# Sums of squares in transposed 32-blocks on VectorE, and factors spread by DMA, in a two-layer trunk on one core

## The chip, the cores and the metric

One core of one Trainium2 chip. The metric is device time in microseconds, the median of the runs. The kernel before takes 2295.11 us (three runs, 2294.74 to 2296.44).

## The reference

Two layers over 512 rows of width 2048, all in float32. Each layer normalises h, multiplies by one wide projection, feeds its columns to three mixers (latent attention A, sparse attention B, differential attention C), gates their outputs, multiplies by an output projection, and adds a gated embedding. The change is about the inner RMS norms: those of the two latents of mixer A, and that of each of the five heads of mixer C.

```python
def rms_norm(x, g):
    y = xf * lax.rsqrt(jnp.mean(xf * xf, axis=-1, keepdims=True) + NORM_EPS)
    return (y * g.astype(jnp.float32)).astype(x.dtype)
...
    q = (rms_norm(c_q, q_norm_g) @ w_uq).reshape(b, s, A_HEADS, A_NOPE + A_ROPE)
    kv = (rms_norm(c_kv, kv_norm_g) @ w_ukv).reshape(b, s, A_HEADS, A_NOPE + A_V)
...
    o = rms_norm(o, subln_g) * (1.0 - lam_init)
```

## The kernel before

Activations lie transposed: features on the 128 partitions, the 512 rows of the sequence (tokens) along the free axis. A norm over features is therefore a sum over partitions. Every float32 operand of a large product is split into a high part (ScalarE, L260 or L263) and a low part (VectorE, L261 or L264), and each product is three matmuls (`mm3`, L358 to L360).

The main loop runs over 15 groups of columns of the input projection (L931). Each group reads its weights in 8 chunks (`chunk`, L338): a DMA on the queue of SyncE (SP) into one of 3 buffers `wr`, then splits into `wh` and `wl` (4 buffers each). The mixers are Python generators that `pump` (L400) steps between the products of a group, by a budget in microseconds that each `yield` states. A scheduler then sets the order of the instructions on each engine by its own timeline; each engine executes its list in that order, and so does each DMA queue.

The square norms are made so. `col_sums` (L308) takes a 128x512 tile of squares and multiplies each 128x128 block of it, as the stationary operand, with two columns of ones: 4 matmuls of float32, each two instructions. The sums come out with the token on the partition. `rsqrt` (L316) makes 1/sqrt of them by ScalarE's Sqrt and a Newton step on VectorE. `spread` (L330) transposes a broadcast of each of the 4 columns, 4 more matmuls, and leaves in PSUM a 128x512 tile with the factor of each token in every partition.

Seven such norms stand in a layer. `latents` (L650) does one for cq (three tiles) and one for ckv (two tiles): squares, `col_sums`, `rsqrt`, `spread`, then z times the factor (L666) and a split with the gain (L667, which runs L263 and L264). The products with `w_uq` (L696) use cq, those with `w_ukv` (`nope_key` and the values, L700 to L717) use ckv. For mixer C, `diff_after` (L825) copies the column sums of each head into `csum`, and after the fifth head takes `rsqrt` of all 20 columns. `gate` (L900) reads a head's output back from DRAM (L905) and multiplies by `spread` of its 4 columns (L908), many groups later.

The queue of GpSimd (POOL) carries the writes to DRAM, that of SP the weights and the reads back. Tiles of 128x512 come from a pool of 59 slots (`slot`); `at` is one of four PSUM banks.

```python
        def latents(kind, n, size, gain, res):
...
            yield GAP
            r = sm(4)
            rsqrt(r, col_sums(total), 4, size)
            yield 0.45
            yield GAP
            rb = spread(r)
            for j in range(n):
                DVE.tensor_tensor(zs[j], zs[j], rb, op=ALU.mult)
                res.append(split(zs[j], col(gain + j)))
```

Of the kernel before, what the change touches and what calls it, by code (L numbers as in the profile page):

```python
# [24 lines left out]
EPS = 1e-6  # L25
# [173 lines left out]
def trunk(ctx: ExitStack, tc: tile.TileContext, t, out):  # L199
# [53 lines left out]
    identb = const.tile([128, 128], BF16, name="identb")  # L253
    DVE.tensor_copy(identb, identf)
    onesf = const.tile([128, 2], F32, name="onesf")
    DVE.memset(onesf, 1.0)
# [47 lines left out]

    mean = const.tile([128, 4 * C_H], F32, name="mean")
    corr = const.tile([128, 4 * C_H], F32, name="corr")

# [7 lines left out]

    def rsqrt(dst, src, n, size):  # L316

        y, m, e = dst[:, :n], mean[:, :n], corr[:, :n]
        o = 0
        for x in src if isinstance(src, list) else [src]:  # L320
            DVE.tensor_scalar(mean[:, o:o + x.shape[1]], x, 1.0 / size, EPS, op0=ALU.mult, op1=ALU.add)
            o += x.shape[1]
# [262 lines left out]
    for L in range(DEPTH):  # L585
# [24 lines left out]
        def take(nm):  # L610
            nonlocal wi
            kind, j = nm
            if kind in ("vb", "vc", "v5"):
# [9 lines left out]
                if kind == "v5":  # L623
                    wi = const.tile([128, NB, 8], F32, name=f"wi{L}")
                    for b in range(NB):
                        DVE.tensor_scalar(wi[:, b], z[nm][b][:, 256:264], rcol[:, b:b + 1], None, op0=ALU.mult)
# [21 lines left out]


        def latents(kind, n, size, gain, res):  # L650
            zs = [raw.pop((kind, j)) for j in range(n)]
# [7 lines left out]
            yield GAP  # L659
            r = sm(4)  # L660
            rsqrt(r, col_sums(total), 4, size)
            yield 0.45
            yield GAP
            rb = spread(r)
            for j in range(n):
# [125 lines left out]

        csum = const.tile([128, 4 * C_H], F32, name=f"csum{L}")

        def diff_needs(x):
# [30 lines left out]
        def diff_after(x, s):  # L825
            DVE.tensor_copy(csum[:, 4 * x:4 * x + 4], col_sums(s))
            yield 0.45
            if x == C_H - 1:
                rsqrt(csum, csum, 4 * C_H, 128)
                done.add(("csum", 0))  # L830

# [68 lines left out]
        def gate(kind, x):  # L900
# [5 lines left out]
            if kind == "gc":  # L906
                finish(("csum", 0))
                DVE.tensor_tensor(o, o, spread(csum[:, 4 * x:4 * x + 4]), op=ALU.mult)  # L908
                DVE.scalar_tensor_tensor(o, o, sub_c[:, L:L + 1], s, op0=ALU.mult, op1=ALU.mult)
            else:  # L910
                DVE.tensor_tensor(o, o, s, op=ALU.mult)
# [194 lines left out]
```

## Time and profile before

| | |
|---|---|
| runs, median (lowest to highest) | 2295.11 us (2294.74 to 2296.44) |
| profiled execution, its own time | 2295.42 us |
| its span, first to last instruction | 2293.6 us |
| granted TensorE clock, mean | 0.997 |
| busy: TensorE (PE), its weight loads (PEld) | 2272.2 us, 1913.0 us |
| busy: VectorE (DVE), ScalarE (ACT), GpSimd (POOL) | 1366.9 us, 1006.9 us, 114.9 us |
| DMA | 268.33 MB, mean 117 GB/s |

A busy share is the time in which an engine had an instruction under way. Durations of matmuls in the profile overlap, since matmuls are pipelined: what one costs is read from the distance between starts, not from its duration. In a timeline each row has its start and its duration in us from the start of the span, and in square brackets how long the engine was idle before it and for whom. "Landing" is the time from a DMA's issue to its last byte.

### The profile page before, as it was taken

The page shows a single profiled execution, that of the slowest core. Times are in us where ns is not written, and L with a number is a line of the kernel's source. Part 1 is how long each engine was busy: PE and PEld are TensorE (multiplying, and loading weights), DVE is VectorE, ACT ScalarE, POOL GpSimd, SP SyncE. Part 2 cuts the span into 40 slices and gives each one's busy share as a digit, 9 for nine tenths or more (in the row PEclk, how much of TensorE's full clock was granted, in tenths as well). Part 3 has the DMA queues.
Part 4 walks back from the last instruction along what each step waited for, and adds up shares of the span by engine and source line. Part 5 has one row for each costly group of instructions (what it writes and reads, how often), then busy time and mean ns, then how long its engine had stood idle before and what let it go on. Part 6 is the DMA issues. An engine that isn't in the chain of part 4 may idle for free.

```text
span 2293.6 us, 29988 instructions
## 1 busy us (share of the span) xinstructions
PE 2272.2 (99%) x10988; PEld 1913.0 (83%) x10988; DVE 1366.9 (60%) x2886; ACT 1006.9 (44%) x1931; POOL 114.9 (5%) x204
## 2 busy tenths in 40 slices
PE   8999999999999999999999999999999999999997
PEld 7898888888888888888888888888888888888887
DVE  7655559977767543344555555699676665333445
ACT  6444445454545432233434444444554454223444
POOL 0000000000000011000000000000000000110003
PEclk9999999999999999999999999999999999999998
DMA  6233323323334345344332333233232243553235
GB/s 201 70 99 116 113 79 96 111 93 97 97 101 161 106 139 185 126 134 136 128 96 76 101 120 104 83 97 102 97 106 102 88 165 115 170 174 130 100 102 165
DMA packets 95220, 268.33 MB, mean 117 GB/s; under 512 B 10976, under 2 KB 26848, under 8 KB 95072
## 3 DMA queue, kind: packets, MB, share of 16 engines
q1 hardware_dynamic: 81760, 223.41, 30.5%
q0 software_dynamic: 13312, 43.00, 5.5%
q8 instruction: 86, 1.41, 0.3%
q14 instruction: 62, 0.51, 0.1%
HBM read 235.96 MB, written 30.41 MB: 116 GB/s over the span
## 4 chain that ended last, share of the span: by engine, by line
PE 98%; ACT 0%; issue 0%; DMA 0%; POOL 0%; SPq 0%; DVE 0%; POOLq 0%; ACTq 0%
PE pp L358 28%; PE pp L359 28%; PE pp L360 28%; PE at L360 3%; PE at L359 3%; PE at L358 3%; PE at L564 2%; PE at L365 1%; PE at L364 1%; PE at L313 1%; PE at L334 0%; DMA x<-in_x_dram 0%; PE at L853 0%; POOL g L1044 0%; ACT wh L260 0%
## 5 line engine op out<-in xcount | busy, mean ns | idle before, releaser
L261 DVE TENSOR_TENSOR wl<-wr,wh 128x512 fp32r<-128x512 f32 (+4 forms) x810 | 530.5, 660 | 731.4 <-ACT wh L260 671.2
L358 PE MATMUL pp<-g,wh 128*128 128x512 f32 (+1 forms) x2432 | 936.0, 386 | 6.2 <-ACT g L263 5.7
L359 PE MATMUL pp<-g,wh 128*128 128x512 f32 (+1 forms) x2432 | 936.1, 385 | 0.0
L260 ACT ACTIVATE wh<-wr 128x512 fp32r<-128x512 f32 (+4 forms) x810 | 487.1, 605 | 978.3 <-PE pp L359 723.9
L360 PE MATMUL pp<-g,wl 128*128 128x512 f32 (+1 forms) x2432 | 911.7, 386 | 0.0
L358 PEld LDWEIGHTS pp<-g,wh 128*128 128x128 f32 x2432 | 457.7, 188 | 94.1 <-ACT g L263 5.7
L359 PEld LDWEIGHTS pp<-g,wh 128*128 128x128 f32 x2432 | 457.6, 188 | 87.5
L360 PEld LDWEIGHTS pp<-g,wl 128*128 128x128 f32 x2432 | 456.7, 188 | 88.6
L359 PE MATMUL pp<-wl,g 128*128 128x512 f32 (+1 forms) x384 | 136.3, 357 | 0.0
L360 PE MATMUL pp<-wh,g 128*128 128x512 f32 (+1 forms) x384 | 135.7, 355 | 0.0
L358 PE MATMUL pp<-wh,g 128*128 128x512 f32 (+1 forms) x384 | 129.3, 363 | 1.2 <-ACT wh L260 1.2
L548 ACT ACTIVATE e<-at,sm 128x128 f32<-128x128 f32 (+3 forms) x128 | 67.0, 525 | 49.5 <-DVE sm L547 48.3
L358 PEld LDWEIGHTS pp<-wh,g 128*128 128x128 f32 x384 | 71.1, 188 | 11.5 <-ACT wh L260 2.1
L360 PEld LDWEIGHTS pp<-wh,g 128*128 128x128 f32 x384 | 72.2, 188 | 9.9
L359 PEld LDWEIGHTS pp<-wl,g 128*128 128x128 f32 x384 | 72.3, 188 | 9.1
L547 DVE TENSOR_REDUCE sm<-at 128x1 f32<-128x128 f32 (+3 forms) x168 | 77.2, 481 | 2.0
L646 POOL DMA_DIRECT2D o_d<-t x32 | 17.4, 542 | 1099.6 <-ACT t L644 1099.6
L261 DVE TENSOR_TENSOR tl<-at,th 128x512 fp32r<-128x512 f32 (+3 forms) x128 | 54.3, 483 | 16.8 <-ACT th L260 16.8
L365 PE MATMUL at<-g 128*128 128x512 f32 (+3 forms) x176 | 53.9, 324 | 0.0
L364 PE MATMUL at<-g 128*128 128x512 f32 (+3 forms) x176 | 53.7, 323 | 0.0
L260 ACT ACTIVATE th<-at 128x512 fp32r<-128x512 f32 (+3 forms) x128 | 45.5, 440 | 18.2 <-PE at L564 18.0
L564 PE MATMUL at<-identf,e 128*128 128x128 f32 x320 | 51.9, 273 | 0.0
(224 smaller groups left out, 2405.2 us busy)
## 6 DMA issues: line engine op xcount, KB each, us to landing
wr<-in_w_in_dram SPq DMA_DIRECT2D x207, 512.0 KB, 3.6
wr<-in_w_pg_dram SPq DMA_DIRECT2D x72, 512.0 KB, 3.7
wr<-in_w_o_dram SPq DMA_DIRECT2D x64, 512.0 KB, 3.7
o_d<-t POOLq DMA_DIRECT2D x32, 256.0 KB, 2.3
g<-o_d SPq DMA_DIRECT2D x32, 256.0 KB, 4.3
hm_d<-t POOLq DMA_DIRECT2D x32, 256.0 KB, 3.2
wr<-in_w_in_dram SPq DMA_DIRECT2D x18, 256.0 KB, 2.6
wr<-in_w_in_dram SPq DMA_DIRECT2D x16, 264.0 KB, 2.6
```

Source lines behind the costliest of these rows:

```text
L260: ACT.activation(hi, src, AF.Copy)
L261: DVE.tensor_tensor(lo, src, f32(hi), op=ALU.subtract)
L313: PE.matmul(ps[:, 2 * b:2 * b + 2], y[:, 128 * b:128 * b + 128], onesf, start=True, stop=True)
L358: PE.matmul(ps, l[0], r[0], start=start, stop=False)
L359: PE.matmul(ps, l[0], r[1], start=False, stop=False)
L360: PE.matmul(ps, l[1], r[0], start=False, stop=stop)
L364: PE.matmul(ps, q[:, qs], k[0][:, :n], start=start, stop=False)
L365: PE.matmul(ps, q[:, qs], k[1][:, :n], start=False, stop=stop)
L547: DVE.tensor_reduce(st[:, 1:2], ps[:, :n], op=ALU.max, axis=AX.X, negate=True)
L548: ACT.activation(e, ps[:, :n], AF.Exp, bias=st[:, 1:2], accum_out=st[:, 2:3])
L564: PE.transpose(ps[:, 128 * (i - kb):128 * (i - kb) + 128], probs[:, BO[i] + 128 * kb:BO[i] + 128 * kb + 128], identf)
L646: nc.gpsimd.dma_start(odram[m], o)
```

## The change

`fold` replaces `col_sums` for the seven inner norms of a layer: VectorE sums each 32x32 block of the squares over rows with a reduce that transposes 32-blocks, which leaves a 128x16 tile; one product with a 128x32 matrix of four stacked identities (`folded`, made once) adds the four groups of 32 partitions. The sums come out as 32x16, and `rsqrt` works on that shape. `put_row` writes the 512 factors to a row in DRAM on POOL's queue, element by element (step 32 in the row), and `get_row` reads the row into all 128 partitions on SP's queue. So `spread` goes from these norms as well. The norms of h and the last norm keep `col_sums` and `spread`. The sums and factors of the five heads are held in one slot in place of `csum`, one row in DRAM each, and are written out after the fifth head.

```diff
@@ -252,6 +252,8 @@
     make_identity(nc, identf)
     identb = const.tile([128, 128], BF16, name="identb")
     DVE.tensor_copy(identb, identf)
+    folded = const.tile([128, 32], F32, name="folded")
+    DVE.tensor_reduce(folded, identf.rearrange("p (a j) -> p j a", j=32), op=ALU.add, axis=AX.X)
     onesf = const.tile([128, 2], F32, name="onesf")
     DVE.memset(onesf, 1.0)
 
@@ -302,8 +304,8 @@
             ACT.activation(s, src, AF.Square)
             DVE.tensor_tensor(acc, acc, s, op=ALU.add)
 
-    mean = const.tile([128, 4 * C_H], F32, name="mean")
-    corr = const.tile([128, 4 * C_H], F32, name="corr")
+    mean4 = const.tile([128, 4], F32, name="mean")
+    corr4 = const.tile([128, 4], F32, name="corr")
 
     def col_sums(y):
 
@@ -313,12 +315,21 @@
             PE.matmul(ps[:, 2 * b:2 * b + 2], y[:, 128 * b:128 * b + 128], onesf, start=True, stop=True)
         return ps[:, 0:2 * nb:2]
 
-    def rsqrt(dst, src, n, size):
-
-        y, m, e = dst[:, :n], mean[:, :n], corr[:, :n]
+    def fold(s):
+
+        part = small.tile([128, 16], F32, name="part", tag="part", bufs=2)
+        DVE.tensor_reduce(part, s.rearrange("p (b j) -> p b j", j=32), op=ALU.add, axis=AX.X, apply_transpose=True)
+        ps = at()
+        PE.matmul(ps[0:32, 0:16], folded, part, start=True, stop=True)
+        return ps[0:32, 0:16]
+
+    def rsqrt(dst, src, n, size, mean=mean4, corr=corr4):
+
+        rows = slice(0, dst.shape[0])
+        y, m, e = dst[:, :n], mean[rows, :n], corr[rows, :n]
         o = 0
         for x in src if isinstance(src, list) else [src]:
-            DVE.tensor_scalar(mean[:, o:o + x.shape[1]], x, 1.0 / size, EPS, op0=ALU.mult, op1=ALU.add)
+            DVE.tensor_scalar(mean[rows, o:o + x.shape[1]], x, 1.0 / size, EPS, op0=ALU.mult, op1=ALU.add)
             o += x.shape[1]
         ACT.activation(y, m, AF.Sqrt)
         DVE.reciprocal(y, y)
@@ -621,7 +632,7 @@
                         nc.gpsimd.dma_start(vdram[to][:, b, c0:c0 + size], r[:, o:o + size])
                         o += size
                 if kind == "v5":
-                    wi = const.tile([128, NB, 8], F32, name=f"wi{L}")
+                    wi = work.tile([128, NB, 8], F32, name="wi", tag="wi", bufs=1)
                     for b in range(NB):
                         DVE.tensor_scalar(wi[:, b], z[nm][b][:, 256:264], rcol[:, b:b + 1], None, op0=ALU.mult)
             elif kind in ("ga", "gb", "gc"):
@@ -647,6 +658,18 @@
             done.add(("out", m))
 
 
+        row_d = {k: dram.tile([1, 512], F32, name=f"row{L}_{k}", tag=f"row{L}_{k}") for k in ("cq", "ckv", 0, 1, 2, 3, 4)}
+
+        def put_row(r, d):
+
+            nc.gpsimd.dma_start(bass.AP(tensor=d.tensor, offset=d.offset, ap=[[1, 32], [32, 16]]), r)
+
+        def get_row(d):
+
+            o = slot()
+            nc.sync.dma_start(o, bass.AP(tensor=d.tensor, offset=d.offset, ap=[[0, 128], [1, 512]]))
+            return o
+
         def latents(kind, n, size, gain, res):
             zs = [raw.pop((kind, j)) for j in range(n)]
             total = slot()
@@ -657,11 +680,13 @@
                 if j:
                     DVE.tensor_tensor(total, total, s, op=ALU.add)
             yield GAP
-            r = sm(4)
-            rsqrt(r, col_sums(total), 4, size)
-            yield 0.45
+            c = slot()
+            r = c[0:32, 0:16]
+            rsqrt(r, fold(total), 16, size, c[:, 16:32], c[:, 32:48])
+            yield 0.25
+            put_row(r, row_d[kind])
+            rb = get_row(row_d[kind])
             yield GAP
-            rb = spread(r)
             for j in range(n):
                 DVE.tensor_tensor(zs[j], zs[j], rb, op=ALU.mult)
                 res.append(split(zs[j], col(gain + j)))
@@ -789,8 +814,7 @@
             done.add(("bias", 0))
 
 
-        csum = const.tile([128, 4 * C_H], F32, name=f"csum{L}")
-
+        norms = {}
         def diff_needs(x):
             return [("kc", x), ("vc" if x < 4 else "v5", 0)]
 
@@ -823,11 +847,17 @@
             return s
 
         def diff_after(x, s):
-            DVE.tensor_copy(csum[:, 4 * x:4 * x + 4], col_sums(s))
-            yield 0.45
+            if x == 0:
+                norms["c"] = slot()
+            c, n = norms["c"], 16 * C_H
+            r = c[0:32, :n]
+            DVE.tensor_copy(r[:, 16 * x:16 * x + 16], fold(s))
+            yield 0.25
             if x == C_H - 1:
-                rsqrt(csum, csum, 4 * C_H, 128)
-                done.add(("csum", 0))
+                rsqrt(r, r, n, 128, c[:, n:2 * n], c[:, 2 * n:3 * n])
+                for y in range(C_H):
+                    put_row(r[:, 16 * y:16 * y + 16], row_d[y])
+                    done.add(("norm", y))
 
 
         def dsa_needs(x):
@@ -904,8 +934,8 @@
             o = slot()
             nc.sync.dma_start(o, odram[m])
             if kind == "gc":
-                finish(("csum", 0))
-                DVE.tensor_tensor(o, o, spread(csum[:, 4 * x:4 * x + 4]), op=ALU.mult)
+                finish(("norm", x))
+                DVE.tensor_tensor(o, o, get_row(row_d[x]), op=ALU.mult)
                 DVE.scalar_tensor_tensor(o, o, sub_c[:, L:L + 1], s, op0=ALU.mult, op1=ALU.mult)
             else:
                 DVE.tensor_tensor(o, o, s, op=ALU.mult)
```

The change moves instructions in three places that matter below. Rows name tiles with their numbers; line numbers are those of the kernel printed. In the changed kernel L263 is the split of L261 before, L266 that of L264, L332 to L339 are `rsqrt` (L321 to L328 before), L369 to L371 are `mm3` (L358 to L360 before), L691 is z times the factor (L666 before), L356 the load of a weight chunk (L345 before); L321 and L323 are the reduce and the product of `fold`, L670 is the read in `get_row`.

VectorE in layer 0 around the norm of ckv, before, from the second step of Newton on (`at_975` is the spread):

```order
L326 TENSOR_TENSOR corr_99<-corr_99,mean_98 128x4
L261 TENSOR_TENSOR wl_1006<-wr_1003,wh_1005 128x384
L327 TENSOR_SCALAR corr_99<-corr_99 128x4
L261 TENSOR_TENSOR wl_1074<-wr_1071,wh_1073 128x264
L328 TENSOR_TENSOR sm_959<-sm_959,corr_99 128x4
L666 TENSOR_TENSOR z_924<-z_924,at_975 128x512
L666 TENSOR_TENSOR z_926<-z_926,at_975 128x512
```

The same place now (`g_977` is the row that comes by DMA, `at_1045` the product with the third column block of `w_uq`):

```order
L339 TENSOR_TENSOR g_964<-g_964 32x16
L263 TENSOR_TENSOR wl_1080<-wr_1073,wh_1079 128x264
L263 TENSOR_TENSOR wl_1107<-wr_1104,wh_1106 128x384
L546 STREAM_SHUFFLE t_1056<-at_1045 128x512
L547 TENSOR_TENSOR t_1055<-at_1045,cosA_104 128x512
L691 TENSOR_TENSOR z_929<-z_929,g_977 128x512
L691 TENSOR_TENSOR z_931<-z_931,g_977 128x512
L263 TENSOR_TENSOR wl_1111<-wr_1104,wh_1110 128x384
L548 TENSOR_TENSOR t_1056<-t_1056,sinA_105 128x512
L263 TENSOR_TENSOR wl_1131<-wr_1128,wh_1130 128x264
L266 SCALAR_TENSOR_TENSOR g_984<-z_929,cc_75,g_983 128x512
```

The two products z times factor follow the last step of `rsqrt` directly before; now four other instructions stand between, and the products head a list with the split `wl_1131` of the next weights behind them.

TensorE in the changed kernel, at the first users of ckv (`g_983` is the high part of its first tile; the fold of ckv stands 56 rows above the first of them: 27 products of 512 columns with cq, then 28 of 264 columns of the main group, of which the last two are the first rows here):

```order
L369 MATMUL pp_939<-wh_1130,g_171 128x264
L369 MATMUL pp_940<-wh_1130,g_171 128x264
L369 MATMUL at_1114<-g_983,wh_1106 128x512
L369 MATMUL at_1156<-wh_1106,g_983 128x256
L370 MATMUL at_1156<-wl_1107,g_983 128x256
L370 MATMUL pp_937<-wl_1131,g_171 128x264
```

Before, 18 products of 264 columns stood between the column sum and the spread, and 27 with cq and 12 of 264 columns between the spread and the first user. Now 55 products stand between the fold and the first user, and nothing of the norm is on TensorE among them.

SP's queue in the changed kernel at the same place (`g_977` is the row read, the others are weight chunks):

```order
L356 DMA wr_1128<-in_w_in_dram 128x528
L356 DMA wr_1179<-in_w_in_dram 128x528
L670 DMA g_977<-row0_ckv_111 128x512
L356 DMA wr_1230<-in_w_in_dram 128x528
L356 DMA wr_1301<-in_w_in_dram 128x528
```

The row read is new between two loads of weights; it waits for the write of the row, and what stands behind it waits with it.

## Rows read from the trace of the kernel before

**Rows 1.** The page, parts 1 and 4: busy time; chain that ended last.

```profile
PE 2272.2 (99%) x10988; PEld 1913.0 (83%) x10988; DVE 1366.9 (60%) x2886; ACT 1006.9 (44%) x1931; POOL 114.9 (5%) x204
PE 98%; ACT 0%; issue 0%; DMA 0%; POOL 0%; SPq 0%; DVE 0%; POOLq 0%; ACTq 0%
```

**Rows 2.** Waits of PE over the whole span: us in total, times, longest.

```profile
PE pp L358 <- ACT wh L260: 1.7, 3, 0.6
```

**Rows 3.** Timeline of PE around the first column sum: start us, us, engine, line.

```profile
68.12 0.95 PE L313 MATMUL at<-onesf,g 128*128 128x2 f32 x8
68.93 0.49 PE L360 MATMUL pp<-g,wl 128*128 128x512 f32 x1
69.25 0.40 PE L359 MATMUL pp<-g,wh 128*128 128x512 f32 x1
```

**Rows 4.** Timeline of PE around the first spread.

```profile
75.42 0.60 PE L334 MATMUL at<-identf,sm 128*128 128x128 f32 x4
75.78 0.48 PE L359 MATMUL pp<-g,wh 128*128 128x512 f32 x1
76.09 0.40 PE L360 MATMUL pp<-g,wl 128*128 128x512 f32 x1
```

**Rows 5.** Lines L313, L334: duration ns min/median/max, first and last start.

```profile
L313 PEld LDWEIGHTS at<-onesf,g x112: 187/192/192, 67.9 to 1756.0; 128*128 128x128 f32 x112
L334 PE MATMUL at<-identf,csum x40: 271/273/292, 691.0 to 1886.3; 128*128 128x128 f32 x40
```

**Rows 6.** Timeline of PE, latent ckv: column sum, first products, first user.

```profile
100.96 0.95 PE L313 MATMUL at<-onesf,g 128*128 128x2 f32 x8
105.47 0.48 PE L358 MATMUL at<-g,wh 128*128 128x512 f32 x1
111.69 0.28 PE L358 MATMUL pp<-wh,g 128*128 128x264 f32 x1
113.13 0.39 PE L358 MATMUL at<-g,wh 128*128 128x512 f32 x1
```

**Rows 7.** Timeline of DVE over the same stretch.

```profile
101.95 0.16 DVE L321 TENSOR_SCALAR mean<-at 128x4 f32<-128x4 f32 x1 [1.53 <-PE at L313]
103.02 0.56 DVE L261 TENSOR_TENSOR wl<-wr,wh 128x384 fp32r<-128x384 f32 x1
103.57 0.43 DVE L261 TENSOR_TENSOR wl<-wr,wh 128x264 fp32r<-128x264 f32 x1
103.91 0.16 DVE L328 TENSOR_TENSOR sm<-sm,corr 128x4 f32<-128x4 f32 x1
105.75 1.29 DVE L666 TENSOR_TENSOR z<-z,at 128x512 f32<-128x512 f32 x2 [1.68 <-PE at L334]
```

**Rows 8.** Groups by line: the high half of a scaled latent on ACT.

```profile
L263 ACT ACTIVATE g<-z,cc 128x512 fp32r<-128x512 f32 x26 | 18.2, 713 | 6.9 <-DVE z L666 6.5
```

**Rows 9.** DMA issues by line: KB each, median us from issue to landing.

```profile
vc_d<-z POOLq DMA_DIRECT2D x8, 64.0 KB, 3.7
```

**Rows 10.** Line L621, POOL's writes of values to DRAM, 64 and 256 KB.

```profile
DMA to landing us min/median/max: 2.3/3.2/5.9
```

**Rows 11.** Line L905, SP's reads of a head's output, 256 KB.

```profile
DMA to landing us min/median/max: 2.8/4.3/6.3
```

**Rows 12.** Line L547, DVE's reduce along a row, 128 to 512 columns.

```profile
L547 DVE TENSOR_REDUCE sm<-at x168: 236/456/693, 122.1 to 1871.9; 128x1 f32<-128x128 f32 x42, 128x1 f32<-128x256 f32 x42, 128x1 f32<-128x384 f32 x42, 128x1 f32<-128x512 f32 x42
```

**Rows 13.** Timelines of DVE and SP: norm of five heads, first gated read.

```profile
625.36 0.18 DVE L321 TENSOR_SCALAR mean<-csum 128x20 f32<-128x20 f32 x1
639.96 0.86 SPq L905 DMA_DIRECT2D g<-o_d  x2
```

**Rows 14.** Timeline of PE at the program's start.

```profile
5.75 2.07 PE L358 MATMUL pp<-g,wh 128*128 128x512 f32 x4 [5.75 <-ACT g L263]
10.18 0.62 PE L359 MATMUL pp<-g,wh 128*128 128x512 f32 x1
10.61 0.43 PE L360 MATMUL pp<-g,wl 128*128 128x512 f32 x1
```

## The prediction

> **What bounds the kernel now.** I read the page first: TensorE is busy for 99% of the span, and the chain that ended last runs over it for 98% [rows 1]. Then the waits of TensorE, where a kernel so full shows its gaps: apart from the start (5.75 us until the first operands are there) the main products waited 1.7 us for weights, in three places [rows 2, 14]. VectorE and ScalarE have room on the whole [rows 1]. So a product less on TensorE is time less, one for one, as long as no new wait on TensorE takes its place. The change is to be costed in two columns: starts that go from TensorE's list, and waits that a longer way for the factors brings.
>
> **What goes.** What a matmul costs is the distance to the next start, not its duration. The column sum starts at 68.12 us and the next product at 68.93, so it takes 0.81 us. The product after that follows at a distance of 0.32 us [rows 3], where a stream of 512-column products has 0.23 (27 of them from 105.47 to 111.69 [rows 6]): another 0.09, since the weight load of the first large product hides behind almost nothing. Together 0.90 us. The spread goes from 75.42 to 75.78, and 0.31 - 0.23 = 0.08 follows it [rows 4]: 0.44 us. One norm thus costs 1.34 us of TensorE. There are 14: 112 instructions of column sums at 8 each, each with a spread (40 transposes of the heads are ten of them at 4) [rows 5]. 14 x 1.34 = 18.8 us.
>
> **What comes on TensorE.** One product of a 128x32 stationary operand with 16 columns, two instructions in float32. The nearest row is the column sum itself, 0.81 / 8 = 0.10 us an instruction with 128 stationary columns, so 0.20 and the same 0.09 behind it are the upper bound, 0.29 us; the lower is the 0.09 alone. I take 0.25, near the upper one, as the number of instructions is certain and the saving by the narrower operand is not seen in any row. 14 x 0.25 = 3.5 us (1.3 to 4.1). Gain on TensorE: 18.8 - 3.5 = 15.3 us (14.7 to 17.5).
>
> The weight load of a column sum takes 192 ns for 128 columns [rows 5]. The Trainium skill (TensorE: Matmul & The Clock Gate, LDWEIGHTS) lets a load grow with the columns alone, at the columns over 1.2 in ns, which is 107 ns here: the row is longer, and the row decides. By its proportion, a quarter of the load for 32 columns, the fold would cost some 0.15 us and the whole some 1.4 us less, an estimate that no row here can show.
>
> **What comes on VectorE.** One reduce of 128x512 for each norm. Along a row such a reduce takes up to 0.69 us [rows 12]; a transposing one is not in the trace. Its bounds are that and double it, 1.4 us. I put it at nothing: for ckv VectorE sat idle for 1.53 us right before it took up the sums [rows 7], and over the whole run for 40% of the time [rows 1]. If it took over 1.5 us, the fold would wait on TensorE for the rest. The steps of `rsqrt` on 32x16 or 32x80 stay short instructions.
>
> **What the longer way costs.** Before, the factors went from VectorE to TensorE and back. Now they go by a write on POOL's queue and a read on SP's. I call the two landings T. The write: POOL's smallest, 64 KB, lands 3.7 us after issue by the median [rows 9], with 2.3 to 5.9 for the line [rows 10]. It moves rows of 512 bytes where the new one moves 512 elements of 4 bytes; nothing in the trace is like that. The read: 256 KB, as the reads of a head's output, 4.3 by the median, 2.8 to 6.3 [rows 11]. I take the medians, T = 8.0 us, as kind and size of the read are the same and the write has its nearest row there; the ends are 5.1 and 12.2.
>
> For **the heads** T is hidden: the norm of all five is taken at 625 us and the first gated read issues at 640 [rows 13]; five writes in between have some 14 us. The read on SP then costs an issue and no wait.
>
> For **cq** it is nearly hidden. Its first user is the `w_uq` block, 138 products after the fold. But the products z times factor stand in VectorE's list, and a split of weights stands behind them whose product is 67 places after the fold, 67 x 0.23 = 15.4 us. The chain of `rsqrt` ended 104.07 - 100.96 = 3.1 us after the start of the column sum [rows 6, 7], and the fold is 0.6 us shorter: 2.5 us. With T, three products of 0.65 and the split of 0.69, the split is done 5.1 + T after the fold. It is late from T = 10.3 on.
>
> For **ckv** it is not hidden. From the fold to the first user TensorE now has 27 products of 0.23 and 28 of 0.12 (12 took 1.44 us, from 111.69 to 113.13 [rows 6]): with the fold's 0.2, 9.8 us. The chain needs 2.5 for `rsqrt` with the two splits inside it [rows 7], T, 0.65 for the first product z times factor [rows 7], 0.71 for its high half on ScalarE [rows 8]: 3.9 + T, 11.9 us. TensorE waits 2.1 us. Then comes a backlog: from the landing VectorE has two products (1.29 us), a split of 384 columns (0.56), a rope step of the same size as one of them (0.65) and the split of 264 columns (0.43) [rows 7], 2.9 us in all, until `wl_1131` is there. TensorE wants it for the fourth product from the first user on, 0.23 + 0.12 + 0.12 us after that one, so 1.36 + 0.47 us after the landing: another 1.1 us. 3.2 us a layer, in general T - 4.8. What SP holds back meanwhile are weights two chunks ahead, whose 48 products of 0.12 us give them some 6 us to spare. Two layers: 6.4 us.
>
> **The sum.** 2295.4 of the profiled execution, less 15.3, plus 6.4: 2286.5. That execution is 0.3 us above the median of the runs, so the forecast is **2286 us**, 0.4% faster.
>
> **The rivals.** *The short way.* If the write lands as the fastest of its line and the read too, T = 5.1 and ckv waits 0.3 us a layer: 2295.1 - 15.3 + 0.6 = 2280.4. For it speaks that only 2 KB are written; against it, that both ends at once are rare, and that 512 pieces are more than any write of the line has. The Trainium skill (DMA: Bandwidth & Descriptors, Anatomy of one DMA) gives 2.0 us fixed and one more for each 436 thousand bytes, which would be 2.0 and 2.6 us, an estimate below any pair of rows here; by that rule it is this case.
>
> *The long way, slower than before.* The 512 elements of 4 bytes make the write as slow as the slowest of its line and the read meets the weights: T = 12.2. Then ckv waits 7.4 us a layer and cq 1.9, 18.6 in all, 3.3 more than the gain: 2298.4. After a wait TensorE may also run slowly for a while. After its 5.75 us of idle at the start, products still stand 0.43 us apart, not 0.23, at 10.61 us [rows 14]: 4.9 us at about half the pace, some 2 us lost for a stop of that kind, and with two stops 2302. The turn comes where T - 4.8, and T - 10.3 if positive, and the 2 us make up 7.7 us a layer: T = 10.5 with the slow restart, 11.4 without. Against it speaks that both medians lie far lower. The Trainium skill (DMA: Bandwidth & Descriptors, Rules for kernel authors) warns of exactly this shape, a last dimension that is not contiguous becoming a descriptor for each element; by that rule this case gains, but it states no time.
>
> *Nothing comes of it.* The freed places on TensorE only show waits for weights that VectorE and ScalarE deliver as late as before; then the time stays at 2295. Against it: 1.7 us of such waits in the whole run [rows 2].
>
> **The chances.** The forecast's mechanism, with T from 6 to 9.5 us: 0.54; its own range is 2282 to 2289. The short way 0.15, the long way or slow restarts 0.22, nothing 0.09. A measurement of this kernel tells about 0.2%, 4.6 us, from no change. The first two cases are faster by more than that: 0.69. Of the long way only its far end, T near 12 with slow restarts, is slower by more: 0.08. The rest is within 0.2%: 0.23. The range reaches from the short way, 2280, to T of 11 with two slow restarts, 2297, and leaves out the far end and folds cheaper than I took them.
>
> **What would show it.** Right: TensorE has some 15 us less work under L313 and L334 in the inner norms; its waits gain two of 2 to 5 us, at the first user of ckv in each layer, released by ScalarE or by a split on VectorE behind the row read; VectorE's z product waits for the row's DMA. The write should land in 3 to 5 us and the read in 4 to 5. Wrong: no such wait on TensorE (short way); waits at cq too, a split of weights as releaser in many places, or products 0.43 us apart behind a wait (long way); a fold that costs over 0.3 us, or one that waits for its reduce.

## The result, and the profile after

The changed kernel takes 2309.36 us, the median of six runs (2307.45 to 2311.61), against 2295.44 for the kernel before in the same six rounds: a ratio of 1.0062, with a 95% interval of 1.0051 to 1.0072. It is slower by 13.9 us. The forecast was 2286, and the range, 2280 to 2297, does not hold it. The profiled execution took 2307.45 us; its span is 2305.7.

The first part of its page, busy time by engine, beside [rows 1]:

```profile
PE 2267.5 (98%) x10838; PEld 1901.2 (82%) x10848; DVE 1376.2 (60%) x2901; ACT 1003.2 (44%) x1931; POOL 123.8 (5%) x218
```

TensorE has fewer instructions and less busy time than before, and yet the span is 12.1 us longer. So the loss stands in waits. The waits of TensorE, beside [rows 2]: us in total, times, longest.

```profile
PE at L369 <- ACT g L265: 11.7, 2, 6.1
PE pp L369 <- ACT g L265: 6.5, 1, 6.5
PE at L575 <- DVE e L886: 5.7, 2, 2.9
```

The second row is the start, as before. The first is new and stands where the forecast had it, at the first user of the ckv latent of each layer, but at 6.1 and 5.6 us where it had 2.1, with 1.1 more behind it. The third is new and nobody had it: a transpose of attention weights that waits for VectorE, 2.9 us, once a layer, at the gates of the heads. Now the DMA issues of the new transfers and of the reads of head outputs: KB each, median us from issue to landing.

```profile
g<-o_d SPq DMA_DIRECT2D x32, 256.0 KB, 4.6
...
g<-row SPq DMA_DIRECT2D x10, 256.0 KB, 5.1
...
g<-row_cq SPq DMA_DIRECT2D x2, 256.0 KB, 4.2
g<-row_ckv SPq DMA_DIRECT2D x2, 256.0 KB, 3.6
...
row<-g POOLq DMA_DIRECT2D x10, 2.0 KB, 12.6
row_cq<-g POOLq DMA_DIRECT2D x2, 2.0 KB, 7.0
row_ckv<-g POOLq DMA_DIRECT2D x2, 2.0 KB, 8.2
```

The reads take 3.6 to 5.1 us by the median, where 4.3 was forecast. The writes, 2 KB each, are the slowest transfers of the whole list. T, the sum of the two landings, is 8.2 + 3.6 = 11.8 us for ckv and 11.2 for cq. Line by line, all the row writes (L665, first row) and the reads of head outputs (L935, second row; [rows 11] is the same line before):

```profile
DMA to landing us min/median/max: 7.0/8.2/22.5
```

```profile
DMA to landing us min/median/max: 2.9/4.6/20.0
```

A read of a head's output now takes up to 20.0 us, where 6.3 was the longest. That is the trace of the second wait. The timeline of the first layer's ckv latent, VectorE and queues (start us, us, engine, line; in brackets the idle time before and what ended it):

```profile
103.73 0.67 POOL L665 DMA_DIRECT2D row_ckv<-g  x1 [29.40 <-DVE g L339]
...
115.80 1.29 DVE L691 TENSOR_TENSOR z<-z,g 128x512 f32<-128x512 f32 x2 [6.63 <-DMA g<-row_ckv]
```

and TensorE there:

```profile
101.02 0.28 PE L371 MATMUL pp<-wh,g 128*128 128x264 f32 x1
101.23 0.23 PE L323 MATMUL at<-part,folded 128*32 128x16 f32 x2
101.39 0.50 PE L369 MATMUL at<-g,wh 128*128 128x512 f32 x1
101.73 0.39 PE L370 MATMUL at<-g,wh 128*128 128x512 f32 x1
...
117.30 0.80 PE L369 MATMUL at<-g,wh 128*128 128x512 f32 x1 [6.12 <-ACT g L265]
...
119.17 0.42 PE L370 MATMUL pp<-wl,g 128*128 128x264 f32 x1
119.39 0.42 PE L371 MATMUL pp<-wh,g 128*128 128x264 f32 x1
```

The fold takes 0.16 us to the next start, and the product behind it stands 0.34 from its successor instead of 0.23: 0.27 together. The product ahead of it counts too: the fold starts 0.21 us after it, where products of 264 columns stand 0.12 apart. That makes 0.36 us, against 0.25 in the forecast and 0.29 as its upper bound. Ahead of the column sum before there was no such gap, 0.12 us from this product to the sum at 100.96 [rows 6]:

```profile
100.84 0.28 PE L360 MATMUL pp<-wh,g 128*128 128x264 f32 x1
```

Behind the wait of 6.12 us the products of 264 columns stand 0.22 us apart, where [rows 6] has 0.12: TensorE runs slowly after it has stood still. The windows of the same stretch (busy time by engine; at the end granted clock, DMA share, GB/s) say so too:

```profile
110.00:120.00 10.00, 3.83 (x19) 3.24 (x19) 4.20 (x8) 2.61 (x5) 0.00 (x0) 0.82 0.36 66
120.00:130.00 10.00, 10.00 (x69) 9.62 (x68) 7.11 (x14) 4.84 (x10) 0.00 (x0) 0.84 0.19 54
```

At the gates of the heads, first layer, the queues first:

```profile
638.77 3.25 POOL L665 DMA_DIRECT2D row<-g  x5 [22.21 <-DVE g L339]
...
641.12 0.86 SPq L935 DMA_DIRECT2D g<-o_d  x2
...
681.10 0.38 SPq L670 DMA_DIRECT2D g<-row  x1
```

then VectorE:

```profile
657.97 0.69 DVE L941 TENSOR_TENSOR g<-g,z 128x512 f32<-128x512 f32 x1 [5.27 <-DMA g<-o_d]
...
661.59 0.69 DVE L941 TENSOR_TENSOR g<-g,z 128x512 f32<-128x512 f32 x1 [2.21 <-DMA g<-o_d]
662.20 1.68 DVE L558 TENSOR_REDUCE sm<-at 128x1 f32<-128x128 f32 x4
```

and TensorE:

```profile
664.52 0.30 PE L575 MATMUL at<-identf,e 128*128 128x128 f32 x1 [2.88 <-DVE e L886]
```

The five rows are written in one burst from 638.77 on. The reads that SP issues 2.4 us later arrive late, VectorE stands before two gates of ordinary heads (L941, no row in them at all) for 5.27 and 2.21 us, and the softmax steps behind them in its list (L558) are late for TensorE. Not one of these instructions waits for a row, and the first read of a row is issued only at 681.10, 40 us behind the late reads. What they share with the rows is the DMA engines. Windows of the changed kernel:

```profile
640.00:650.00 10.00, 10.00 (x50) 8.44 (x49) 8.63 (x17) 4.63 (x8) 2.59 (x5) 1.00 1.04 41
650.00:660.00 10.00, 10.00 (x49) 8.16 (x49) 3.46 (x6) 3.79 (x5) 0.00 (x0) 1.00 0.89 113
660.00:670.00 10.00, 7.07 (x29) 5.34 (x28) 7.41 (x20) 5.26 (x15) 0.00 (x0) 0.83 0.62 162
```

In the ten microseconds from 640 the 16 engines are busy throughout by the profile (share 1.04) and move 41 GB/s. In the window with the stop of TensorE the granted clock is 0.83. The kernel before, in the same stretch, moved 181 GB/s at a share of 0.54:

```profile
640.00:650.00 10.00, 10.00 (x50) 8.14 (x49) 7.25 (x18) 6.33 (x14) 0.00 (x0) 1.00 0.54 181
```

### The profile page after: what moved, and what is told of

The parts are those of the page before. It is cut to its first block, busy times and chain, and to the rows that moved or that the text cites. A ratio compares the mean times of both kernels' runs of the same rounds, so it can differ in the third digit from the quotient of the medians.

```text
span 2305.7 us, 29784 instructions
## 1 busy us (share of the span) xinstructions
PE 2267.5 (98%) x10838; PEld 1901.2 (82%) x10848; DVE 1376.2 (60%) x2901; ACT 1003.2 (44%) x1931; POOL 123.8 (5%) x218
## 4 chain that ended last, share of the span: by engine, by line
PE 90%; issue 5%; DMA 3%; DVE 1%; POOL 0%; ACT 0%; SPq 0%; POOLq 0%; DVEq 0%; ACTq 0%
PE pp L369 26%; PE pp L370 26%; PE pp L371 26%; PE at L370 3%; PE at L371 3%; PE at L369 3%; DMA g<-o_d 2%; PE at L575 2%; PE at L376 1%; PE at L375 1%; DMA row_ckv<-g 1%; DMA g<-row_ckv 0%; DMA row_cq<-g 0%; DVE wl L263 0%; DMA g<-row_cq 0%
## 5 line engine op out<-in xcount | busy, mean ns | idle before, releaser
L369 PE MATMUL pp<-g,wh 128*128 128x512 f32 (+1 forms) x2432 | 936.4, 386 | 6.5 <-ACT g L265 6.5
L263 DVE TENSOR_TENSOR wl<-wr,wh 128x512 fp32r<-128x512 f32 (+4 forms) x810 | 528.8, 659 | 686.0 <-ACT wh L262 633.6
L371 PE MATMUL pp<-g,wl 128*128 128x512 f32 (+1 forms) x2432 | 914.6, 386 | 1.1 <-DVE wl L263 1.1
L369 PEld LDWEIGHTS pp<-g,wh 128*128 128x128 f32 x2432 | 458.3, 189 | 94.0 <-ACT g L265 6.5
L371 PEld LDWEIGHTS pp<-g,wl 128*128 128x128 f32 x2432 | 457.0, 188 | 90.5 <-DVE wl L263 2.8
L371 PE MATMUL pp<-wh,g 128*128 128x512 f32 (+1 forms) x384 | 136.7, 358 | 0.0
L369 PE MATMUL pp<-wh,g 128*128 128x512 f32 (+1 forms) x384 | 128.4, 365 | 0.0
L371 PEld LDWEIGHTS pp<-wh,g 128*128 128x128 f32 x384 | 73.3, 191 | 9.7
L369 PEld LDWEIGHTS pp<-wh,g 128*128 128x128 f32 x384 | 71.0, 191 | 9.5 <-ACT wh L262 0.5
L558 DVE TENSOR_REDUCE sm<-at 128x1 f32<-128x128 f32 (+3 forms) x168 | 76.1, 479 | 1.6
L263 DVE TENSOR_TENSOR tl<-at,th 128x512 fp32r<-128x512 f32 (+3 forms) x128 | 54.1, 483 | 21.7 <-ACT th L262 21.6
L575 PEld LDWEIGHTS at<-identf,e 128*128 128x128 f32 x320 | 40.7, 142 | 16.4 <-ACT e L559 6.5
L376 PE MATMUL at<-g 128*128 128x512 f32 (+3 forms) x176 | 54.2, 324 | 0.0
```

The source lines that it names most:

```text
L263: DVE.tensor_tensor(lo, src, f32(hi), op=ALU.subtract)
L369: PE.matmul(ps, l[0], r[0], start=start, stop=False)
L371: PE.matmul(ps, l[1], r[0], start=False, stop=stop)
L376: PE.matmul(ps, q[:, qs], k[1][:, :n], start=False, stop=stop)
L558: DVE.tensor_reduce(st[:, 1:2], ps[:, :n], op=ALU.max, axis=AX.X, negate=True)
L575: PE.transpose(ps[:, 128 * (i - kb):128 * (i - kb) + 128], probs[:, BO[i] + 128 * kb:BO[i] + 128 * kb + 128], identf)
```

## The experiments

**The theory (A)**: the shape of the row's write is the cost. 512 elements of 4 bytes, each 128 bytes from the one before it in the same partition, land slowly, which makes ckv wait; and they hold the DMA engines, which makes other transfers late. The gain on TensorE is there as forecast. **The rivals**: (B) a trip through DRAM costs this much in any shape; (C, E) the loss at the heads comes from where the row reads stand in SP's queue and what they wait for; (D) the fold or the reduce eats the gain; (F) every element row costs, wherever it stands.

### The two halves apart

The latents as before, the heads as changed:

```
-            c = slot()
-            r = c[0:32, 0:16]
-            rsqrt(r, fold(total), 16, size, c[:, 16:32], c[:, 32:48])
...
-            put_row(r, row_d[kind])
-            rb = get_row(row_d[kind])
+            r = sm(4)
+            rsqrt(r, col_sums(total), 4, size)
...
+            rb = spread(r)
```

> Edit: the four latent norms (cq and ckv of two layers) keep the column sums and the spread of the kernel before; the ten head norms are as changed. Measured so far: the changed kernel is 13.9 us over the one before; in its trace the products fall behind by 8.0 us (first layer) and 6.1 us (second) around the ckv latent, gain 1.0 at each cq latent, and come out even over the five heads of a layer (5 us gained in folds and spreads, 5 to 8 lost when the five rows are written in one burst). Theory A (a row of 512 elements of 4 bytes is a slow write that also holds the DMA engines): the ckv loss goes, the burst stays: 2309.4 - 14.1 + 2.0 = 2297.3 us, 2294 to 2300; the waits of TensorE for the first use of the ckv latent gone, the wait of a score product behind the gate of a head (2.9 us, twice) still there. Rival B (any trip through DRAM takes 7 to 8 us to land, whatever the shape of the row): the same here. Rival D (the fold or the transposing reduce eats the gain on TensorE): no fold pays, the heads lose by themselves: 2300 to 2306 us, with falling behind at each of the five folds.

Measured: 2295.19 us, ratio 0.9997 (0.9988 to 1.0005). Waits of TensorE:

```profile
PE at L575 <- DVE e L884: 5.0, 2, 2.8
```

The ckv wait is gone and the wait at the gates is there, as A has it (B has the same for this run). D's 2300 and more is refuted: ten folds and spreads pay for the two bursts. The time is 2.1 us below A's sum, near the lower end of its range. One reason is seen: the stop at the gates of the first layer is 2.1 us here, and the granted clock of its window stays at 1.00, where the changed kernel has 0.83.

```profile
650.00:660.00 10.00, 7.82 (x39) 6.05 (x38) 6.79 (x19) 4.26 (x13) 0.00 (x0) 1.00 0.59 132
```

The heads as before, the latents as changed:

```
-            DVE.tensor_copy(r[:, 16 * x:16 * x + 16], fold(s))
+            DVE.tensor_copy(c[:, 4 * x:4 * x + 4], col_sums(s))
...
-                    put_row(r[:, 16 * y:16 * y + 16], row_d[y])
...
-                DVE.tensor_tensor(o, o, get_row(row_d[x]), op=ALU.mult)
+                DVE.tensor_tensor(o, o, spread(norms["c"][:, 4 * x:4 * x + 4]), op=ALU.mult)
```

> Edit: the ten head norms keep the column sums and the spread (factors held in one tile of the slot pool instead of three small ones); the four latent norms are as changed. Theory A: the heads of a layer come out even in the changed kernel, gain and burst against each other, so without both the time stays: 2309.4 us, 2306 to 2312, the two ckv losses (8.0 and 6.1 us) still in the trace, the DMA share around the gates of the heads back from 1.04 to about 0.5, and no wait of a score product there. A theory by which the ckv loss comes only from the order of work or of tile slots that the head norms changed: 2295 us or less.

Measured: 2306.03 us, 1.0047 (1.0034 to 1.0059), at the lower end of what A gave.

```profile
PE at L369 <- ACT g L265: 10.1, 2, 5.1
```

```profile
row_ckv<-g POOLq DMA_DIRECT2D x2, 2.0 KB, 7.4
```

The ckv waits stay without the heads' change, the wait at the gates goes. So the ckv loss does not come from the order of work that the heads' change brought, which would have given 2295 or less. The two halves cost nothing and 10.8 us against before, and the whole costs 13.9. Of the 3.1 us between, 1.6 are seen: the ckv waits add up to 10.1 us here and 11.7 in the whole. Why the same writes land 0.8 us sooner here was not traced.

### The same transfers in another shape

Everything as changed, but the factors are turned on VectorE, so that 16 runs of 128 bytes leave:

```
-            nc.gpsimd.dma_start(bass.AP(..., ap=[[1, 32], [32, 16]]), r)
+            nc.gpsimd.dma_start(bass.AP(..., ap=[[32, 16], [1, 32]]), r)
...
-            put_row(r, row_d[kind])
+            DVE.transpose(c[0:32, 64:96], c[0:32, 0:32])
+            put_row(c[0:16, 64:96], row_d[kind])
...
+                DVE.transpose(c[0:32, 256:352], c[0:32, 0:96])
                 for y in range(C_H):
-                    put_row(r[:, 16 * y:16 * y + 16], row_d[y])
+                    p, o = 16 * (y % 2), 256 + 32 * (y // 2)
+                    put_row(c[p:p + 16, o:o + 32], row_d[y])
```

> Edit: everything as changed, but the factors are turned by a 32x32 transpose on VectorE ahead of the write, so that a row goes out as 16 runs of 128 bytes instead of 512 elements of 4 bytes; the number of transfers, their queues and places stay. Theory A (the elements are the cost): the write lands in 2 to 4 us instead of 7 to 8, the round trip takes 6 to 8 us, the wait at the ckv latent falls from 6 us to 1 to 3 us a layer, the DMA share at the gates of the heads falls from 1.04 to about 0.5 and the wait of the score product there is gone: 2281 to 2288 us. Rival B (the trip through DRAM, whatever its shape): write landing still 7 us and more, 2307 to 2311 us. Rival C (the row reads that stand on the SP queue ahead of the reads of head outputs make the loss at the gates, by their place in the queue): the ckv loss shrinks, the loss at the gates stays: 2294 to 2300 us.

Measured: **2281.61 us**, 0.9940 (0.9927 to 0.9952): 27.75 us below the changed kernel and 13.6 below the one before. A alone has this, and the result is better than A said, which left 1 to 3 us of wait at ckv in each layer. Left are 0.5 and 0.4 us, for a split of weights behind the first user:

```profile
PE pp L370 <- DVE wl L263: 0.9, 2, 0.5
```

The landings:

```profile
row<-g POOLq DMA_DIRECT2D x10, 2.0 KB, 3.3
row_ckv<-g POOLq DMA_DIRECT2D x2, 2.0 KB, 1.6
```

The same 2 KB to the same place land in 1.6 to 3.3 us by the median instead of 7.0 to 12.6. The ckv latent in VectorE's and the queues' timeline:

```profile
103.43 0.49 POOL L665 DMA_DIRECT2D row_ckv<-g  x1 [27.73 <-DVE g L687]
105.33 0.38 SPq L670 DMA_DIRECT2D g<-row_ckv  x1
108.81 1.29 DVE L692 TENSOR_TENSOR z<-z,g 128x512 f32<-128x512 f32 x2 [0.16 <-DMA g<-row_ckv]
```

From the write's issue to the use of the row it is 5.4 us, against 12.1 (103.73 to 115.80) in the changed kernel. At the gates the DMA share is back (the window answers to the one with 1.04):

```profile
640.00:650.00 10.00, 10.00 (x50) 8.15 (x49) 7.84 (x20) 6.62 (x14) 0.00 (x0) 1.00 0.44 131
```

B is refuted by the landing. C is refuted because the row reads stand in the same places of SP's queue and no wait at the gates is left; in the changed kernel they are issued after the late reads anyway.

The same with the ckv latents by the way of before, since theirs are the only factors that are used at once:

```
+            if kind == "ckv":
+                r = sm(4)
+                rsqrt(r, col_sums(total), 4, size)
...
+                rb = spread(r)
+            else:
```

> Edit: as the kernel with runs of 128 bytes, but the ckv latent of each layer keeps the column sums and the spread of the kernel before (its factors are the only ones that are used at once). Theory A: 12 norms gain 1.0 us each, nothing waits: 2295.4 - 12 + 0.8 = 2284 us, 2281 to 2287; below the kernel with runs of 128 bytes by what is left of its ckv wait less the 2 us that its two ckv folds and spreads gain. Rival B: the ckv loss is gone, the rows of the heads still land late: 2295 to 2300 us. Rival C: the same, 2294 to 2300 us.

Measured: 2284.77 us, 0.9954 (0.9940 to 0.9967), 3.2 above the kernel with runs everywhere, where 2 was expected for two folds and spreads. TensorE waits 2.3 us for high halves of weights here and 0.9 us for low halves there, which is 1.4 of the 3.2. So with a short T even ckv pays, 1.6 us a layer: the long way there is nearly hidden, and it should not be taken out.

And with the operands of the fold exchanged, so that the sums come out as 16 rows of 32 and need no turning:

```
-        PE.matmul(ps[0:32, 0:16], folded, part, start=True, stop=True)
+        PE.matmul(ps[0:16, 0:32], part, folded, start=True, stop=True)
```

The cut shows the product alone. The write has the destination of the kernel with runs, and `rsqrt` works on 16x32 for a latent and 16x160 for the heads.

> Edit: as changed, but the two operands of the folding product change places: the partial sums are the weights (128x16) and the matrix of blocks is streamed (32 columns), so the sums come out as 16 rows of 32, and a row of factors goes out as 16 runs of 128 bytes without a transpose on VectorE. Theory A (the shape of the write is all that was wrong): as the kernel that turned the factors on VectorE, 2281.6 us, 2280 to 2283: less work on VectorE, a weight load of 16 columns instead of 32, and 16 streamed columns more for each of 14 folds. If the streamed columns cost more than the weight load saves: up to 0.1 us a fold, 2283.

Measured: 2281.70 us, 0.9940 (0.9927 to 0.9952), with the write at 1.6 us for ckv and 3.7 for the heads. The line of the fold, weight load and product (duration ns min/median/max):

```profile
L323 PEld LDWEIGHTS at<-folded,part x28: 91/94/97, 71.0 to 1746.6; 128*16 128x16 f32 x28
L323 PE MATMUL at<-folded,part x28: 193/198/204, 71.0 to 1746.7; 128*16 128x32 f32 x28
```

With the fold as changed, in the kernel with the transposes, the medians are 108 and 192 ns: the load is 14 ns shorter, the product 6 longer. The time is the same, and this form needs no instruction more than the change itself.

### Writes that nobody reads

To see the hold on the DMA engines by itself, the kernel before got five writes a layer behind the factors of the heads, to rows that are never read:

```
                 rsqrt(csum, csum, 4 * C_H, 128)
                 done.add(("csum", 0))
+                for y in range(C_H):
+                    d = dram.tile([1, 512], F32, name=f"row{L}_{y}", tag=f"row{L}_{y}")
+                    nc.gpsimd.dma_start(bass.AP(..., ap=[[1, 32], [32, 16]]), csum[0:32, 0:16])
```

> Edit: the kernel before, with five writes of 512 elements of 4 bytes a layer added behind the factors of the heads, on POOL's queue, to rows that nobody reads. Nothing waits for them by data. Theory A (the elements hold the DMA engines, and the reads of head outputs that gates wait for come late): the wait of VectorE for a head output grows to 5 us and more, a score product waits for VectorE, DMA share about 1 behind the writes; 5 us lost a layer: 2295.2 + 10 = 2305 us, 2302 to 2309. Rival E (the loss at the heads in the changed kernel comes from the wait of the row reads for their writes, and what is queued behind them on SP): nothing waits here, 2294.5 to 2296.5 us.

Measured: 2308.82 us, 1.0049 (1.0035 to 1.0063). Ten writes of 2 KB that no instruction waits for cost 13 us (8 to 14 by the interval). VectorE's waits for head outputs, before (L911) and here (L914), and TensorE's wait behind them:

```profile
DVE g L911 <- DMA g<-o_d: 6.3, 5, 1.8
```

```profile
DVE g L914 <- DMA g<-o_d: 25.3, 5, 11.9
```

```profile
PE pp L360 <- DVE wl L261: 7.2, 2, 4.8
```

VectorE waits for head outputs up to 11.9 us, and a split of weights behind such a gate makes TensorE wait, 7.2 us in all. Around the first of these waits the granted clock falls again, to 0.83 from 650 to 660. (A had a score product as the one that is late; which it is depends on what stands behind the gate.) E is refuted. The control has the same source, the same bytes and the same queue, and only the destination differs, 32 runs of 64 bytes:

```
+                    nc.gpsimd.dma_start(bass.AP(..., ap=[[16, 32], [1, 16]]), csum[0:32, 0:16])
```

> Edit: the kernel before with the same five idle writes a layer of the same bytes, but as 32 runs of 64 bytes each. Theory A: the number of pieces is what holds the engines, so nearly nothing is left: 2295.2 us, 2294.5 to 2297. If five more transfers on POOL's queue are the cost, whatever their pieces: as the kernel with idle elements, 2302 to 2309 us.

Measured: 2296.30 us, 1.0003 (0.9994 to 1.0012). Landing of the ten writes, elements first, runs second:

```profile
DMA to landing us min/median/max: 7.2/12.1/19.1
```

```profile
DMA to landing us min/median/max: 1.6/1.6/1.6
```

and the windows at the gates, with elements:

```profile
630.00:640.00 10.00, 10.00 (x49) 8.45 (x48) 8.05 (x15) 5.54 (x9) 2.03 (x4) 1.00 0.89 37
640.00:650.00 10.00, 10.00 (x49) 8.14 (x49) 1.90 (x3) 3.95 (x7) 0.00 (x0) 1.00 0.93 95
```

and with runs:

```profile
630.00:640.00 10.00, 10.00 (x49) 8.47 (x48) 7.84 (x16) 5.54 (x9) 1.84 (x4) 1.00 0.24 80
640.00:650.00 10.00, 10.00 (x48) 8.12 (x49) 7.25 (x14) 6.51 (x14) 0.00 (x0) 1.00 0.53 168
```

In these 20 us the engines are busy for 18.2 us with the elements under way and for 7.7 with the runs, other transfers included. What about the shape is slow stays open. The elements are more pieces, and neighbours in the row come from different partitions; no run separates the two, and none issues the element writes from another queue than POOL's.

### The burst taken apart

Latents as before, and each head's row of elements written when that head is folded:

```
-            DVE.tensor_copy(r[:, 16 * x:16 * x + 16], fold(s))
...
+            rsqrt(r, fold(s), 16, 128, c[:, o + 16:o + 32], c[:, o + 32:o + 48])
             yield 0.25
...
+            put_row(r, row_d[x])
+            done.add(("norm", x))
```

> Edit: the kernel with the four latent norms of before (2295.2 us), but each head's factors are finished and its row of 512 elements written as soon as that head is folded, not all five at the end. Theory A: the same elements, but one row at a time, some 10 us and more apart, so only the last row is still under way when the head outputs are read: the 10 us of gain at the heads are seen, 2285 us, 2284 to 2289. Rival F (every element row costs some 1 us wherever it stands): 2293 to 2296 us.

Measured: 2287.72 us, 0.9967 (0.9955 to 0.9980), 7.5 below the kernel with the burst. The landing of the row writes falls from 12.1 to 6.9 us by the median. The same elements one row at a time do little harm where nothing urgent is behind them. (In the first layer they go out 30 to 44 us apart, the last at 629.71.) F is refuted.

## Why the prediction was wrong

For the account, the main products (those into `pp`) of two traces are numbered in order of time and paired by number, and the starts are subtracted. The last column is what the element writes cost against the runs of 128 bytes in that stretch.

| up to product | before | changed | runs of 128 B | changed - before | runs - before | lost in the stretch |
|---|---|---|---|---|---|---|
| 300, before the first cq factors are used | 79.76 | 78.30 | 78.69 | -1.46 | -1.07 | |
| 400, before the first ckv | 100.72 | 100.18 | 99.66 | -0.54 | -1.06 | 0.9 |
| 1800, ckv used | 496.51 | 502.52 | 493.49 | +6.01 | -3.02 | 8.5 |
| 2900, heads and gates | 796.47 | 803.36 | 789.32 | +6.89 | -7.15 | 5.0 |
| 6000, latents of layer two | 1596.51 | 1609.47 | 1586.85 | +12.96 | -9.66 | 8.6 |
| 7200, heads of layer two | 1923.10 | 1936.09 | 1908.84 | +12.99 | -14.26 | 4.6 |

**The products on TensorE: right in kind, the fold priced too low.** 14 norms were to give 15.3 us, 14.7 at the least. The kernel with runs, where only 0.9 us of waits is left, is 14.26 us ahead at the end of its heads. Its later start (0.8 us) is not in this: by main product 50 the two kernels are level, 20.27 and 20.22 us. The fold was taken at 0.25 us and takes 0.36 at ckv, as the gap ahead of it had no term; 14 x (1.34 - 0.36) gives 13.7. A fold over 0.3 us was among the prediction's own signs of being wrong, but these 1.5 us do not turn a gain into a loss. The reduce was put at nothing with bounds of 0.69 and 1.4; the row of the changed kernel has 0.707 us, and its trace has no wait of TensorE that the reduce ends:

```profile
L321 DVE TRANSPOSE_TENSOR_REDUCE part<-g 128x16 f32<-128x512 f32 x14 | 9.9, 707 | 2.4 <-ACT g L845 2.3
```

**The landing of the write: wrong, the first step that failed.** It was taken at 3.7 us, "as kind and size of the read are the same and the write has its nearest row there". The read had a row of its kind and came out at 3.6 for ckv, below the 4.3. The write had none: the row it was read from moves runs of 512 bytes, and the prediction said so and took its median all the same. Measured is 8.2 us for ckv, above 5.9, the end of the bounds. With the shape corrected the write lands in 1.6 to 3.7 us by the median. A price whose nearest row differs in the one property that the change brings in has no upper end from that row.

**The formula for ckv, T - 4.8: right in form.** With T = 11.8 it gives 7.0 us: 5.9 of wait at the first user and 1.1 of backlog behind it. TensorE waited 6.1 and 5.6 at the first user; the backlog does not show among its waits. In the kernel with runs T = 1.6 + 3.5 = 5.1, and the formula leaves 0.3 us a layer; measured are 0.5 and 0.4. The short way had this T from other parts (2.3 + 2.8), by luck; it gave 2280.4, and 2281.6 was measured. The forecast's 3.2 was this formula with the wrong T. For cq, T - 10.3 gives 0.9 us a layer at T = 11.2. The table has 0.9 in layer one, of which the trace shows 0.3 as a wait of TensorE for a split; layer two is not separated from ckv in the table, and its trace shows 0.8.

**The slow restart: left to a rival, and it came.** The rival put some 2 us on a stop. In layer one ckv lost 8.5 us, of which 6.1 are the wait: 2.4. At the gates 5.0 were lost and 2.9 are the wait: 2.1. The granted clock of 0.82 to 0.84 in the windows shows the same. Not every stop brings it: behind the 2.1 us at the gates in the kernel with the latents as before the clock stayed at 1.00. A forecast that has a wait of 3 us at the first user should carry that term, with a chance.

**"For the heads T is hidden": right, and the second step that failed, since other transfers were put at nothing.** The latency of the five writes is indeed covered: the reads of these rows are issued from 681 us on. What the sentence left out is that a transfer also takes the 16 engines from others. The loss at the gates, 5.0 + 4.6 = 9.6 us, comes from the reads of head outputs behind the burst, and idle writes bring it into the kernel before as well. None of the rivals held this; the long way, priced at up to 2302 us, had the sign and the ckv part. With the measured T and 2 us for each of the two ckv stops, the prediction's own terms give 2295.1 - 15.3 + 2 x (7.0 + 0.9 + 2) = 2299.6, and the missing 9.8 us of 2309.4 are about the loss at the gates.

The table takes the measured difference apart and does not predict it: 2295.42 - 14.26 + (0.9 + 8.5 + 8.6) + 9.6 = 2308.8, against 2307.45 in the profiled execution. Of the 1.3 us between, 0.4 is a lead that the changed kernel has over the one with runs ahead of its first norm, and the rest lies behind the last main product.

The trace decided which of two rules of the Trainium skill bore on this case. Its fit of time to bytes for transfers that GpSimd issues (DMA: Bandwidth & Descriptors, Anatomy of one DMA), by our estimate 2.0 us for so small a write, is near the runs, which landed in 1.6 to 3.7 us by the median, and misses the elements by 5 us and more. The prediction used it for the reads on SP's queue too, 2.6 us, for which it is not stated; they took 3.6 to 5.1. Its warning of a last dimension that is not contiguous (the same page, Rules for kernel authors) is borne out by the pair of idle writes, 1.6 against 7.2 to 19.1 us. That transfers issued by different engines share the same 16 DMA engines stands there too (Issuing engines are not separate DMA queues); the windows agree, with a share of 0.89 to 1.04 behind the burst.

## What to carry to other kernels

Cost a new DMA twice: by its latency at whoever waits for it, and by the time it holds the engines at everyone else's transfers; being hidden from its own reader clears only the first. Write rows from the layout in which they are contiguous: here it took one exchange of two matmul operands (2281.7 us) or a transpose in 32x32 blocks to turn a change that lost 13.9 us into one that gains 13.6. Where the trace has no transfer of the same shape, test the shape alone before building on it, and let the upper bound stay open.

## What was not expected of the hardware

The count of packets does not tell the two shapes apart. The kernel with idle elements and the one with idle runs have the same counts on their pages, and only the mean rate differs, 116 and 117 GB/s. With elements:

```profile
DMA packets 95540, 268.35 MB, mean 116 GB/s; under 512 B 11296, under 2 KB 27168, under 8 KB 95392
```

Yet the one write of 2 KB lands after 1.6 us and the other after at least 7.2. Whoever looks for scattered writes finds them here by landing and by a high DMA share at a low rate, not by packets. Issuing one also takes POOL longer, 0.65 us by the median against 0.50. Further, a run of 64 bytes is no worse than one of 128 here: the idle runs of 64 bytes land in 1.6 us, as the rows of ckv do in runs of 128. And VectorE's transposing reduce of a 128x512 tile costs the same as a reduce along the rows, 0.71 against 0.69 us [rows 12].
